# Where the low parts of split weights begin in SBUF: 64 bytes further for the stationary operand only

## The chip, the core and the metric

The kernel runs on one core of one Trainium2 chip. The time is the device time of one execution in microseconds; a kernel's time is the median over its runs. Three runs of the kernel before gave 1090.84 us at the median, from 1089.98 to 1092.05 us.

## What is computed

Two layers of a sequence model on 256 tokens of width 1024, in float32. Each layer is a half-weighted SwiGLU feed-forward network, a mixer, and another half-weighted feed-forward network, each between RMS norms and with a residual. The mixer of the first layer joins a gated convolution of width 31 with a state-space scan; that of the second is dilated window attention in three groups of eight heads. Nearly all of the arithmetic is products of the 256-token activations with weight matrices:

```python
def swiglu(u, w1, w2):
    gate, up = jnp.split(u @ w1, 2, axis=-1)        # w1: 1024 x 5632
    return (jax.nn.silu(gate) * up) @ w2            # w2: 2816 x 1024
...
for i in range(DEPTH):                              # DEPTH = 2
    h = h + 0.5 * rms_norm(swiglu(rms_norm(h, g[0]), ffn_w1[i, 0], ffn_w2[i, 0]), g[1])
    u = rms_norm(h, g[2])
    m = conv_ssd_mixer(u, ...) if i % 2 == 0 else dilated_attention_mixer(u, ...)
    h = h + rms_norm(m, g[3])
    h = h + 0.5 * rms_norm(swiglu(rms_norm(h, g[4]), ffn_w1[i, 1], ffn_w2[i, 1]), g[5])
```

## The kernel before

The weights lie in HBM as units of 128 x 2048 float32, in the order of their use. `prefetch` (L608) loads a unit into a `raw` buffer, ScalarE copies it to `wh` rounded to the matmul's type fp32r, and VectorE (GpSimd for the units 38 to 54) writes the rest, `raw - wh`, to `wl`. `wh` is the high part, `wl` the low part. Activations are split the same way, so that a product takes three matmuls: high by high, high by low, low by high. There are four buffers each of `raw`, `wh` and `wl`.

A unit is read in one of two ways. `unit(inner)` (L626) hands both parts out as `[128, k, inner]`.

- **As the stationary operand**, where `inner` is 256. `by_parts` (L671) streams high and low part of an activation (512 columns) past a 128 x 128 block of `wh`, and then the high part alone (256 columns) past the block of `wl`. `feat_major` (L661) does the same in three matmuls of 256 columns.
- **As the moving operand**, where `inner` is 512 or 1024. `mm3` (L635) loads a 128 x 128 block of the activation's high part and streams 512 columns of `wh`, loads it again and streams 512 columns of `wl`, and loads the low part and streams `wh` once more. It is called from `tok_major` (L655; activation tiles named `x`) and `acc_pairs` (L687; the down projections, whose activation tiles are named `s`, `x` in the mixer's output). The trace names a matmul's moving operand first: `w<-x,wl` streams `x` past a stationary `wl`, and `a<-wl,s` streams `wl` past a stationary `s`.

Each matmul has a LDWEIGHTS of its own, and the load for the next matmul begins while the current one streams.

All operations are recorded first. A planner (`schedule`, L336) simulates the engines with costs and gives each operation its place in its engine's queue and each buffer its slot; `lay_out` (L442) then creates the large buffers one behind the other, and `issue` (L459) issues everything in the planned order from L466, which is why the profile puts everything at that line. `lay_out` creates all large buffers except those of `wl` first, then one tile of 64 bytes that nothing uses, and then the four `wl` buffers. The small tiles follow as they come up. In the built program every large buffer begins 128 bytes past a multiple of 512, and the four `wl` buffers (at 192192, 200384, 208576 and 216768 in a partition) begin 192 bytes past one: 64 bytes further than all others. Blocks within a buffer are cut at multiples of 512 bytes, so this holds for every operand of the matmuls above. Below, "at 64" is said of an operand that begins there, and "at 0" of one that begins as the others do.

Of the kernel before, what the change touches and what calls it, by code (L numbers as in the profile page):

```python
# [9 lines left out]
F32 = mybir.dt.float32  # L10
# [7 lines left out]
P = 128  # L18
# [146 lines left out]
class View:  # L165


    def __init__(self, buf, ap, path=()):
        self.buf, self.ap, self.path = buf, ap, path
# [27 lines left out]
        return np.unique(at // self.buf.grain).tolist()  # L197


LINE, LINES = 64, 512  # L200


class Buf:
    def __init__(self, kind, shape, dtype, index):
        self.kind, self.shape, self.dtype, self.index = kind, shape, dtype, index
        self.cols = int(np.prod(shape[1:]))
        self.grain = max(1, self.cols // 32)
        self.slot = self.real = None
        self.uses = set()
        self.writer, self.readers, self.users = {}, {}, {}  # L210

    def tile(self):
        if self.real is None:
            k = self.kind
            self.real = k.pool.tile(self.shape, self.dtype, name=f"{k.name}_{self.index}", tag=f"{k.name}{self.slot}", bufs=1)
        return self.real


class Kind:


    def __init__(self, pool, name, count, psum):
        self.pool, self.name, self.count, self.psum = pool, name, count, psum
        self.bufs = []
        self.tenant = {}
        self.first = 0
        self.free_at = [0.0] * count
# [18 lines left out]
class Recorder:  # L246
# [8 lines left out]
        for e in ("tensor", "vector", "scalar", "gpsimd", "sync"):  # L255
            setattr(self, e, Engine(self, e))

    def kind(self, pool, name, count, psum=False):
        self.kinds[name] = Kind(pool, name, count, psum)

    def tile(self, name, shape, dtype=F32):
        kind = self.kinds[name]
        buf = Buf(kind, list(shape), dtype, len(kind.bufs))
        kind.bufs.append(buf)
        return View(buf, self.like(buf.shape, dtype))
# [176 lines left out]
    def lay_out(self, order):  # L442

        first = {}
        for o in order:
            for b in o.bufs:
                if not b.kind.psum:
                    first.setdefault((b.kind.name, b.slot), b)
        size = lambda b: b.cols * mybir.dt.size(b.dtype)
        large = [b for b in first.values() if size(b) % LINES == 0]  # L450
        for b in large:
            if b.kind.name != "wl":
                b.tile()
        next(iter(first.values())).kind.pool.tile([P, LINE // 4], F32, name="line", tag="line", bufs=1)
        for b in large:
            if b.kind.name == "wl":
                b.tile()

    def issue(self):  # L459
        real = lambda a: a.placed() if isinstance(a, View) else a  # L460
        with self.tc.manual_schedule():
            order = self.schedule()
            self.lay_out(order)
            for o in order:
                f = getattr(getattr(self.tc.nc, o.engine), o.name)
                o.ins = f(*[real(a) for a in o.args], **{k: real(a) for k, a in o.kw.items()})  # L466
# [79 lines left out]
class Kernel:  # L546
    def __init__(self, ctx, tc, x, weights, w_dt, gains, chan, heads, dt_bias, consts, out):
        self.tc, self.nc = tc, Recorder(tc)
        self.weights, self.gains = weights, gains
        self.x, self.out = x, out  # L550
        self.n = 0
        self.next_unit = 0
        self.use_unit = 0
        self.units = {}
        self.bg = []
        nc = self.nc
        sb = ctx.enter_context(tc.tile_pool(name="sb", bufs=1))
        ps = ctx.enter_context(tc.tile_pool(name="ps", bufs=1, space=PSUM))
        kind = lambda name, count: nc.kind(sb, name, count)
        kinds = {"raw": RAW_BUFS, "wh": W_BUFS, "wl": W_BUFS, "g": 2, "junk": 2}  # L560
        for name, count in {**kinds, **SB_BUFS, **{f"m{n}": count for n, count in SMALL.items()}}.items():
            kind(name, count)
        for name, count in PS_BUFS.items():
            nc.kind(ps, name, count, psum=True)
        self.kind = kind

        self.h = [self.keep(f"h{t}", [P, D]) for t in range(NT)]
        self.ident = self.keep("ident", [P, P])
        self.order = self.keep("order", [P, 2, P])
        self.consts = consts  # L570
        self.gain0 = self.keep("gain0", [P, KB])
        self.mhalf = self.keep("mhalf", [P, 1])
        nc.gpsimd.memset(self.mhalf, -0.5)
        self.mean = self.keep("mean", [P, P])
        nc.gpsimd.memset(self.mean, 1.0 / D)
        self.chan = self.keep("chan", [P, N_CHAN])
        self.heads = self.keep("heads", [P, 2, 16])
        self.dt_bias = self.keep("dtb", [16, 1])
        self.in_small = (chan, heads, dt_bias, w_dt)
# [46 lines left out]
    def unit(self, inner):  # L626
        i = self.use_unit
        self.use_unit += 1
        self.prefetch(i + 1 + AHEAD)
        hi, lo = self.units.pop(i)  # L630
        r = lambda a: a.rearrange("p (k n) -> p k n", n=inner)
        return r(hi), r(lo)

# [27 lines left out]
    def feat_major(self, ps, xT, unit, blk):  # L661
        hi, lo = unit
        for kb in range(KB):
            w = tuple(a[:, kb, blk * P : (blk + 1) * P] for a in (hi, lo))
            x = self.xb(xT, kb)
            mm = self.nc.tensor.matmul
            mm(ps, w[0], x[0], start=kb == 0, stop=False)
            mm(ps, w[0], x[1], start=False, stop=False)
            mm(ps, w[1], x[0], start=False, stop=kb == KB - 1)

    def by_parts(self, xT, unit, blk, bank, out, scale=1.0):  # L671

        nc = self.nc
        hi, lo = unit
        ps = self.ps([P, 2, SEQ], bank)
        for kb in range(KB):
            w = tuple(a[:, kb, blk * P : (blk + 1) * P] for a in (hi, lo))
            x = xT[kb // 2][:, kb % 2]
            nc.tensor.matmul(ps, w[0], x, start=kb == 0, stop=False)
            nc.tensor.matmul(ps[:, 0, :], w[1], x[:, 0, :], start=False, stop=kb == KB - 1)  # L680
        nc.scalar.activation(out, ps[:, 1, :], AF.Copy, scale=scale)
        if scale == 1.0:
            nc.vector.tensor_tensor(out=out, in0=ps[:, 0, :], in1=out, op=ALU.add)
        else:
            nc.vector.scalar_tensor_tensor(out=out, in0=ps[:, 0, :], scalar=scale, in1=out, op0=ALU.mult, op1=ALU.add)

    def acc_pairs(self, acc, lhs, unit, kk, start, stop, halves=(0, 1), **kw):  # L687
        hi, lo = unit
        for hf in halves:
            c = slice(hf * 512, (hf + 1) * 512)  # L690
            self.mm3(acc[hf], lhs, (hi[:, kk, c], lo[:, kk, c]), start, stop, **kw)
# [728 lines left out]
```

## Time and profile before

| | |
|---|---|
| median of three runs | 1090.84 us |
| the profiled execution's own time | 1091.85 us |
| its span on the core | 1090.1 us |
| TensorE (PE) matmuls, busy | 1072.9 us, 98% |
| weight loads (PEld), busy | 905.3 us, 83% |
| VectorE (DVE), busy | 765.8 us, 70% |
| ScalarE (ACT), busy | 656.4 us, 60% |
| GpSimd (POOL), busy | 142.2 us, 13% |
| 16 DMA engines, mean share | 51.3% (weights' queue) |
| mean granted TensorE clock | 0.999 of full speed |

The profile comes from one execution. Matmuls overlap in the pipeline, so a matmul's duration holds the time in which the next one already streams, and the ends are modelled; how much time one takes up is read from the starts of two of them in the timeline. A row of a group gives the operation, out<-in, the shape, how often it occurs, the busy time in us, the mean duration in ns, and the idle time before it with what ended that.

### The profile page before, as it was taken

To read this page: it belongs to the slowest core of one execution; us is meant where nothing else is said; L and a number is where in the kernel's file an instruction comes from. 1 tells how busy PE (TensorE), PEld (TensorE's weight loads), DVE (VectorE), ACT (ScalarE), POOL (GpSimd) and SP (SyncE) were. 2 spreads that over 40 slices of the span, in tenths; PEclk is the share of its full clock that TensorE was granted. 3 is DMA by queue.
4 is the path that set the end of the run, shared out by engine and by line. 5 is a ranking of instruction groups with operands and counts; after the bars stand their busy time and mean duration, and the time that the engine had idled before them with its cause. 6 is when DMAs were issued, how large, how long until landed. Compare 5 with 4: busy or idle time off the path is not lost.

```text
span 1090.1 us, 15864 instructions
## 1 busy us (share of the span) xinstructions
PE 1072.9 (98%) x5822; PEld 905.3 (83%) x5822; DVE 765.8 (70%) x1574; ACT 656.4 (60%) x1447; POOL 142.2 (13%) x136
## 2 busy tenths in 40 slices
PE   6999999999999999999999999999999999999997
PEld 5888888888878888888888888888888788888886
DVE  6756565889999885666677566568688868566563
ACT  7655555687676664655565555556576656465452
POOL 0000000069896000000000000000000400000000
PEclk9999999999999999999999999999999999999999
DMA  9755555445324576546537465554645235554621
GB/s 346 253 195 187 194 193 193 155 155 194 117 82 150 193 247 216 184 164 215 178 137 281 155 217 176 185 193 136 246 162 193 98 116 207 199 193 160 227 78 39
DMA packets 30206, 196.58 MB, mean 180 GB/s; under 512 B 3632, under 2 KB 4528, under 8 KB 7600
## 3 DMA queue, kind: packets, MB, share of 16 engines
q1 hardware_dynamic: 30128, 195.57, 51.3%
q8 instruction: 45, 0.74, 0.3%
q14 instruction: 33, 0.27, 0.1%
HBM read 194.51 MB, written 1.05 MB: 179 GB/s over the span
## 4 chain that ended last, share of the span: by engine, by line
PE 93%; DVE 3%; ACT 2%; DMA 1%; issue 0%; SPq 0%; DVEq 0%; POOLq 0%; POOL 0%; ACTq 0%
PE w L466 38%; PE a L466 32%; PE t L466 12%; PE c L466 12%; DVE c L466 1%; DVE t L466 1%; ACT wh L466 1%; DMA gain<-in_chan 1%; DVE s L466 0%; ACT junk L466 0%; SPq L466 0%; ACT c L466 0%; ACT t L466 0%; DVE m L466 0%; DVE h L466 0%
## 5 line engine op out<-in xcount | busy, mean ns | idle before, releaser
L466 DVE TENSOR_TENSOR wl<-raw,wh 128x512 fp32r<-128x512 f32 x642 | 415.0, 692 | 164.5 <-ACT wh L466 164.0
L466 ACT ACTIVATE wh<-raw 128x512 fp32r<-128x512 f32 x710 | 405.4, 626 | 205.4 <-PE a L466 83.3
L466 PE MATMUL w<-x,wh 128*128 128x512 f32 (+1 forms) x864 | 266.4, 365 | 0.9 <-DVE pt L466 0.7
L466 PE MATMUL a<-wh,s 128*128 128x512 f32 x800 | 256.4, 394 | 0.0
L466 PE MATMUL w<-x,wl 128*128 128x256 f32 x752 | 210.9, 281 | 0.0
L466 PEld LDWEIGHTS a<-wh,s 128*128 128x128 f32 x800 | 150.1, 188 | 35.8 <-ACT s L466 0.8
L466 PEld LDWEIGHTS w<-x,wh 128*128 128x128 f32 x864 | 154.6, 188 | 28.4 <-DVE pt L466 1.0
L466 PE MATMUL w<-wh,x 128*128 128x512 f32 x512 | 169.5, 405 | 1.9 <-ACT x L466 1.8
L466 PE MATMUL a<-wl,s 128*128 128x512 f32 x400 | 157.7, 394 | 0.0
L466 PEld LDWEIGHTS w<-x,wl 128*128 128x128 f32 x752 | 142.8, 190 | 2.1 <-issue 0.9
L466 POOL TENSOR_TENSOR m<-m,mhalf 128x1 f32<-128x1 f32 x28 | 18.0, 645 | 819.0 <-DVE m L466 818.9
L466 PE MATMUL t<-x,wh 128*128 128x512 f32 x336 | 118.5, 392 | 0.0
L466 PE MATMUL c<-x,wh 128*128 128x512 f32 x336 | 118.4, 392 | 0.0
L466 PEld LDWEIGHTS w<-wh,x 128*128 128x128 f32 x512 | 96.5, 190 | 24.6 <-ACT x L466 2.5
L466 PE MATMUL w<-wl,x 128*128 128x512 f32 x256 | 102.8, 403 | 0.0
L466 PE MATMUL t<-x,wl 128*128 128x256 f32 x336 | 94.0, 280 | 0.0
L466 PE MATMUL c<-x,wl 128*128 128x256 f32 x336 | 93.9, 280 | 0.0
L466 POOL TENSOR_TENSOR wl<-raw,wh 128x512 fp32r<-128x512 f32 x68 | 85.5, 1300 | 23.9 <-ACT wh L466 23.7
L466 PEld LDWEIGHTS a<-wl,s 128*128 128x128 f32 x400 | 75.1, 188 | 16.2
L466 ACT ACTIVATE sg<-w 128x256 f32<-128x256 f32 x96 | 36.6, 381 | 81.2 <-PE w L466 81.2
L466 DVE TENSOR_TENSOR sg<-w,sg 128x256 f32<-128x256 f32 x72 | 30.5, 424 | 78.0 <-ACT sg L466 75.4
L466 PEld LDWEIGHTS c<-x,wh 128*128 128x128 f32 x336 | 63.1, 188 | 13.5
(176 smaller groups left out, 1204.0 us busy)
## 6 DMA issues: line engine op xcount, KB each, us to landing
raw<-in_weights SPq DMA_DIRECT2D x176, 1024.0 KB, 4.8
g<-in_gains SPq DMA_DIRECT2D x11, 512.0 KB, 5.0
raw<-in_weights SPq DMA_DIRECT2D x4, 256.0 KB, 5.8
raw<-in_weights SPq DMA_DIRECT2D x2, 512.0 KB, 7.7
out<-h SPq DMA_DIRECT2D x4, 256.0 KB, 2.0
g<-in_consts SPq DMA_DIRECT2D x3, 192.0 KB, 2.4
h<-in_x SPq DMA_DIRECT2D x2, 256.0 KB, 2.8
h<-in_x SPq DMA_DIRECT2D x1, 512.0 KB, 6.5
```

What stands on the lines that cost most here:

```text
L466: o.ins = f(*[real(a) for a in o.args], **{k: real(a) for k, a in o.kw.items()})
```

## The change

The unused tile of 64 bytes goes. The `wl` buffers become 64 bytes larger (2064 instead of 2048 elements per partition), and each tenant of such a buffer gets a shift of its own: `unit` sets it to 16 elements, 64 bytes, where the unit is handed out with `inner == 256` (stationary) and to 0 otherwise (moving). Writing and reading both go through `Buf.tile`, so both see the shift.

```diff
-LINE, LINES = 64, 512
+LINE, LINES = 16, 512
...
     def tile(self):
         if self.real is None:
             k = self.kind
-            self.real = k.pool.tile(self.shape, self.dtype, name=f"{k.name}_{self.index}", tag=f"{k.name}{self.slot}", bufs=1)
-        return self.real
+            shape = [P, self.cols + k.margin] if k.margin else self.shape
+            self.real = k.pool.tile(shape, self.dtype, name=f"{k.name}_{self.index}", tag=f"{k.name}{self.slot}", bufs=1)
+        return self.real[:, self.shift : self.shift + self.cols] if self.kind.margin else self.real
...
-        size = lambda b: b.cols * mybir.dt.size(b.dtype)
-        large = [b for b in first.values() if size(b) % LINES == 0]
-        for b in large:
-            if b.kind.name != "wl":
+        size = lambda b: (b.cols + b.kind.margin) * mybir.dt.size(b.dtype)
+        small = sorted((b for b in first.values() if size(b) % LINES and not b.kind.margin), key=size, reverse=True)
+        for b in first.values():
+            if size(b) % LINES == 0:
                 b.tile()
-        next(iter(first.values())).kind.pool.tile([P, LINE // 4], F32, name="line", tag="line", bufs=1)
-        for b in large:
-            if b.kind.name == "wl":
+        for b in first.values():
+            if b.kind.margin:
                 b.tile()
+                room = -size(b) % LINES
+                for other in list(small):
+                    if (n := -(-size(other) // 32) * 32) <= room:
+                        other.tile()
+                        small.remove(other)
+                        room -= n
...
-        kind = lambda name, count: nc.kind(sb, name, count)
+        kind = lambda name, count: nc.kind(sb, name, count, margin=LINE if name == "wl" else 0)
...
         hi, lo = self.units.pop(i)
+
+        lo.buf.shift = LINE if inner == 256 else 0
```

In the built program the `wl` buffers now begin at 192128, 200832, 209536 and 218240, each 128 bytes past a multiple of 512, and small tiles (scalars and short rows of 4 to 128 bytes) fill the 448 bytes behind each. A stationary `wl` is read at 64, as before, in 1472 matmuls; a moving `wl` is read at 0 instead of 64, in 688 matmuls. No other large buffer moves. On all five engines the instructions, their order and the semaphores on which they wait are the same as before; addresses alone differ.

More of the change, by code (lines that the diff above doesn't have):

```diff
@@ L208, in __init__ @@
         self.slot = self.real = None
+        self.shift = 0
         self.uses = set()
@@ L214, in tile, with __init__ @@
             k = self.kind
-            self.real = k.pool.tile(self.shape, self.dtype, name=f"{k.name}_{self.index}", tag=f"{k.name}{self.slot}", bufs=1)
-        return self.real
+            shape = [P, self.cols + k.margin] if k.margin else self.shape
+            self.real = k.pool.tile(shape, self.dtype, name=f"{k.name}_{self.index}", tag=f"{k.name}{self.slot}", bufs=1)
+        return self.real[:, self.shift : self.shift + self.cols] if self.kind.margin else self.real
 class Kind:
-    def __init__(self, pool, name, count, psum):
-        self.pool, self.name, self.count, self.psum = pool, name, count, psum
+    def __init__(self, pool, name, count, psum, margin):
+        self.pool, self.name, self.count, self.psum, self.margin = pool, name, count, psum, margin
         self.bufs = []
@@ L256, in __init__, with kind @@
             setattr(self, e, Engine(self, e))
-    def kind(self, pool, name, count, psum=False):
-        self.kinds[name] = Kind(pool, name, count, psum)
+    def kind(self, pool, name, count, psum=False, margin=0):
+        self.kinds[name] = Kind(pool, name, count, psum, margin)
     def tile(self, name, shape, dtype=F32):
```

## The prediction

> **What bounds the kernel now.** I read the page first, for the engine that sets the end.
>
> ```profile
> span 1090.1 us, 15864 instructions
> PE 1072.9 (98%) x5822; PEld 905.3 (83%) x5822; DVE 765.8 (70%) x1574; ACT 656.4 (60%) x1447; POOL 142.2 (13%) x136
> ...
> PE 93%; DVE 3%; ACT 2%; DMA 1%; issue 0%; SPq 0%; DVEq 0%; POOLq 0%; POOL 0%; ACTq 0%
> PE w L466 38%; PE a L466 32%; PE t L466 12%; PE c L466 12%; DVE c L466 1%; DVE t L466 1%; ACT wh L466 1%; DMA gain<-in_chan 1%; DVE s L466 0%; ACT junk L466 0%; SPq L466 0%; ACT c L466 0%; ACT t L466 0%; DVE m L466 0%; DVE h L466 0%
> ```
>
> TensorE is busy for 98% of the span, and 93% of the chain that ended last is matmuls. So a change counts here only by what it does to the time that a matmul takes up in an unbroken stream. Next came the groups of TensorE with their shapes kept apart. These are the matmuls that touch a split weight (some small groups of the mixers left out).
>
> ```profile
> L466 PE MATMUL a<-wh,s 128*128 128x512 f32 x800 | 256.4, 394 | 0.0
> L466 PE MATMUL w<-x,wh 128*128 128x512 f32 x640 | 225.0, 393 | 0.0
> L466 PE MATMUL w<-x,wl 128*128 128x256 f32 x752 | 210.9, 281 | 0.0
> L466 PE MATMUL w<-wh,x 128*128 128x512 f32 x512 | 169.5, 405 | 1.9 <-ACT x L466 1.8
> L466 PE MATMUL a<-wl,s 128*128 128x512 f32 x400 | 157.7, 394 | 0.0
> L466 PE MATMUL t<-x,wh 128*128 128x512 f32 x336 | 118.5, 392 | 0.0
> ...
> L466 PE MATMUL w<-wl,x 128*128 128x512 f32 x256 | 102.8, 403 | 0.0
> ...
> L466 PE MATMUL a<-wh,x 128*128 128x512 f32 x64 | 21.3, 403 | 0.0
> ...
> L466 PE MATMUL a<-wl,x 128*128 128x512 f32 x32 | 12.7, 397 | 0.0
> ```
>
> The reader is to see two things: the groups hardly wait (idle 0.0 to 1.9 us), and the moving `wl`, which the change concerns, occurs 400 + 256 + 32 = 688 times. Durations overlap, so for the time that a matmul takes up I read the timeline of one passage of a feed-forward stage, from a pair of blocks in `by_parts` to the end of the down projection behind it. The rows are the first of `by_parts`, the first and the second of the down projection, and the first behind it.
>
> ```profile
> 82.06 0.39 PE L466 MATMUL t<-x,wh 128*128 128x512 f32 x1
> 82.29 0.28 PE L466 MATMUL t<-x,wl 128*128 128x256 f32 x1
> ...
> 87.61 0.40 PE L466 MATMUL a<-wh,s 128*128 128x512 f32 x1
> 87.84 0.39 PE L466 MATMUL a<-wl,s 128*128 128x512 f32 x1
> ...
> 93.17 0.39 PE L466 MATMUL w<-x,wh 128*128 128x512 f32 x1
> ```
>
> From 82.06 to 87.61 us stand 16 pairs of a 512- and a 256-column matmul: 5.55 us / 16 = 346.9 ns a pair. From 87.61 to 93.17 us stand 24 matmuls of 512 columns, 16 that move `wh` and 8 that move `wl`: 5.56 us / 24 = 231.7 ns each. That is the stretch that the change touches. The 688 moving `wl` take 688 x 231.7 ns = 159 us, 15% of the span, and the triples that they stand in, 3 x 688 matmuls, 478 us.
>
> **The change part by part.**
>
> *The stationary `wl`* stays at 64, in 1472 matmuls, and reads the same data against the same streams: nothing.
>
> *The moving `wl`* goes from 64 to 0, where `wh` lies already. The trace therefore holds both cases side by side, in the same triples, with the same stationary blocks: `a<-wl,s` streams from 64 and takes 394 ns, `a<-wh,s` streams from 0 and takes 394 ns. Both are rounded, so they differ by less than 1 ns. In the tok_major groups the pairs are 403 against 405 and 397 against 403; the `wh` row there holds the first matmul of each group, which has waited (1.9 us of idle time), so these pairs say no more than the first, and I take that one. If a moving `wl` at 0 behaves as `wh` does at 0, the sum is 688 x 0 = 0, with 688 x 1 ns = 0.7 us either way from the rounding.
>
> That is a comparison within a triple, and it leaves one thing open: whether one operand's place costs its neighbour time. So I looked for a row in which only the place of the operands against each other changes. The step sizes in the mixer have one. Their stationary block is 16 columns, 64 bytes, and eight such blocks lie one behind the other in 512 bytes, while 256 columns of `x` stream from 0 each time. The two answers below are for the first two blocks (while they stream, blocks at 0, 64 and 128 are loaded) and for four later ones (loads at 192 to 448), each with minimum, median and maximum of the duration; the maxima of 362 and 360 are the first matmul of each stretch, which has waited.
>
> ```profile
> L466 PE MATMUL w<-x,wdth x4: 282/282/362, 223.4 to 224.0; 128*16 128x256 f32 x4
> L466 PE MATMUL w<-x,wdtl x2: 282/282/283, 223.7 to 224.1; 128*16 128x256 f32 x2
> ...
> L466 PE MATMUL w<-x,wdth x8: 276/276/360, 225.2 to 226.4; 128*16 128x256 f32 x8
> L466 PE MATMUL w<-x,wdtl x4: 276/276/276, 225.5 to 226.5; 128*16 128x256 f32 x4
> ```
>
> The same matmul takes 282 ns with its neighbour's weights at 0 to 128 bytes from the stream's beginning, and 276 ns with them further on. So a load seems to cost the stream up to 6 ns where the two lie close, though a short wait stands between the two stretches and could be the reason instead. A 128-column block is 512 bytes, so its load passes through all eight places whatever it begins with, and a shift can only move the moment at which the two meet. That is why I expect far less than 6 ns of a shift of 64 bytes, and why the equal 394 ns of the two rows don't surprise me.
>
> The Trainium skill, page "TensorE: Matmul & The Clock Gate", section "Step-by-step: what each phase is for", states that TensorE has two independent read ports and that loading the next weights does not steal read bandwidth from the running matmul. By that rule no address changes anything and the sum is exactly 0; the 282 and 276 ns speak against it as a whole. Whether it holds for 128-column blocks no row here decides.
>
> *The bounds.* Below: a 512-column stream in `by_parts`, whose neighbour's load is at 64, takes 392 ns (`t<-x,wh`) against 394 ns in the triples, so an arrangement exists in which it is 2 ns shorter. If the triples' shift against each other is what they pay for, all three matmuls gain: 3 x 688 x 2 ns = 4.1 us less. Above: the step sizes' 6 ns for each moving `wl` that now begins where its neighbour's load begins: 688 x 6 ns = 4.1 us more.
>
> *Writing `wl`.* VectorE and GpSimd now write the moving units to 0.
>
> ```profile
> L466 DVE TENSOR_TENSOR wl<-raw,wh 128x512 fp32r<-128x512 f32 x640 | 412.6, 691 | 164.5 <-ACT wh L466 164.0
> L466 DVE TENSOR_TENSOR s<-cv,s 128x512 fp32r<-128x512 f32 x36 | 24.7, 686 | 0.7 <-ACT s L466 0.7
> ```
>
> The same operation to a tile at 0 takes 686 ns against 691 ns: at most 5 ns less in each of 640 instructions, 3.2 us of VectorE's time for all of them, and under half of that for the units that move. It is covered: these instructions idle for 164.5 us, 164.0 of it waiting for ScalarE's `wh`, and `wl` is not in the chain. Without that cover it would be a gain of some 1 us. Small tiles at new addresses are read by a few short instructions each; nothing in the chain above 1% reads them.
>
> **The sum.** 0 for the stationary parts, 0 +- 0.7 us for the moving ones, 0 for VectorE. The profiled execution took 1091.85 us (span 1090.1), 1.0 us over the median of 1090.84, so the forecast for the median is 1090.84 + 0 = 1090.8 us. A measurement of this kernel can tell about 0.2%, 2.2 us, from no change; 0.7 us is inside that.
>
> **The rivals.**
>
> *Faster: the triple as a whole pays for the shift.* Durations in the down projection are not constant: its matmuls take 387 to 402 ns in one passage although nothing waits, while those of `by_parts` keep to 392 or 393.
>
> ```profile
> L466 PE MATMUL a<-wh,s x15: 387/395/402, 87.6 to 92.5; 128*128 128x512 f32 x15
> L466 PE MATMUL a<-wl,s x8: 388/394/398, 87.8 to 92.7; 128*128 128x512 f32 x8
> ```
>
> So something carries over from one matmul to the next there, and the third operand at 64 in each triple may be what stirs it; in that case equal means of `wh` and `wl` prove nothing, because both share the cost. With all three at 0 the stream could settle at `by_parts`' 392 ns: -4.1 us, 1086.7 us. Against it: `by_parts` itself mixes both places (its load of `wl` at 64, that of `wh` at 0) and is steady.
>
> *Slower: a collision at the beginning of the stream.* While a moving `wl` streams, the block for the next matmul is loaded from 0. Before, the two begin 64 bytes apart; now both begin at 0, and if the load holds the stream up where they begin together, each of 688 matmuls pays up to the 6 ns of the step sizes: +4.1 us, 1094.9 us. It decides from 2.2 us / 688 = 3.2 ns per matmul on. Against it: `wh` at 0 is in that very position in the same triples and shows 394 ns too.
>
> *The change doesn't do what it says:* it would, if a unit with `inner == 256` were moved anywhere or its writer kept another shift. In the built program all 1472 stationary `wl` are at 64 and all 688 moving ones at 0, so I give this nothing beyond the case of no change.
>
> **How the numbers follow.** No measurable change: 0.46, because it is what the paired rows say. Faster: 0.37; the scatter of 387 to 402 ns shows that time is there to be had, and 2 ns on 2064 matmuls is enough. Slower: 0.17, which needs more than half of the price of the step sizes while `wh` already stands in the same place for none. The range goes from 1085.9 us (the faster case and 0.8 us for the scatter of a median) to 1094.0 us (the no-change case with its rounding, and the greater part of the slower one), which leaves about 2 in 10 outside; the no-change case by itself spans 1089 to 1093 us.
>
> **What would show it.** In the profile after, `a<-wl,s` and `a<-wh,s` at 394 ns each, and 5.56 us for a passage of 24 matmuls between two stretches of `by_parts`, would show the forecast right. At 392 ns for both and 5.51 us the faster rival is right, at 400 ns for `wl` alone (5.61 us) the slower. `by_parts` must stay at 346.9 ns a pair, and `w<-x,wl` at 281 ns; if they move, the stationary parts were not left alone. If the span moves and none of these rows does, the reason lies with an engine that I gave nothing.

## The result and the profile after

The changed kernel takes 1084.32 us at the median of six runs (1084.09 to 1085.6), the kernel before 1091.14 us in six runs beside it. The ratio is 0.9939, with a 95% interval from 0.9929 to 0.9949: 6.8 us faster, and below the range that was forecast. The profiled execution took 1084.34 us, against 1091.85 us before. The page of after, in the lines that answer to those of before:

```profile
span 1082.5 us, 15864 instructions
PE 1064.8 (98%) x5822; PEld 903.6 (83%) x5822; DVE 765.1 (71%) x1574; ACT 656.2 (61%) x1447; POOL 142.3 (13%) x136
...
PE 93%; DVE 3%; ACT 2%; DMA 1%; issue 0%; SPq 0%; DVEq 0%; POOLq 0%; POOL 0%; ACTq 0%
```

The span is 7.6 us shorter, TensorE's busy time 8.1 us, and TensorE is still 93% of the chain. Its weight loads (PEld) are 1.7 us shorter; no other engine moved by as much as 1 us. The groups of TensorE in after, with shapes kept apart:

```profile
L473 PE MATMUL a<-wh,s 128*128 128x512 f32 x800 | 253.2, 391 | 0.0
L473 PE MATMUL w<-x,wh 128*128 128x512 f32 x640 | 225.0, 393 | 0.0
L473 PE MATMUL w<-x,wl 128*128 128x256 f32 x752 | 210.9, 281 | 0.0
L473 PE MATMUL w<-wh,x 128*128 128x512 f32 x512 | 167.3, 401 | 2.3 <-ACT x L473 2.2
L473 PE MATMUL a<-wl,s 128*128 128x512 f32 x400 | 156.6, 391 | 0.0
L473 PE MATMUL t<-x,wh 128*128 128x512 f32 x336 | 118.5, 392 | 0.0
...
L473 PE MATMUL w<-wl,x 128*128 128x512 f32 x256 | 101.8, 400 | 0.0
...
L473 PE MATMUL a<-wh,x 128*128 128x512 f32 x64 | 21.1, 400 | 0.0
...
L473 PE MATMUL a<-wl,x 128*128 128x512 f32 x32 | 12.6, 394 | 0.0
```

Two things are to be seen. The groups with a stationary weight (`w<-x,wh`, `w<-x,wl`, `t<-x,wh`) show the same figures as before. And in the triples the moving `wh`, which the change does not touch, got shorter as the moving `wl` did: both go from 394 to 391 ns. The six groups of the triples lose 3.2 + 2.2 + 1.1 + 1.0 + 0.2 + 0.1 = 7.8 us, which accounts for the whole of the span's 7.6 us. The passage of a feed-forward stage in after (first of `by_parts`, first of the down projection, first behind it):

```profile
80.59 0.39 PE L473 MATMUL t<-x,wh 128*128 128x512 f32 x1
...
86.14 0.40 PE L473 MATMUL a<-wh,s 128*128 128x512 f32 x1
...
91.62 0.39 PE L473 MATMUL w<-x,wh 128*128 128x512 f32 x1
```

The 16 pairs take 5.55 us as before, 346.9 ns a pair. The 24 matmuls of the triples take 5.48 us, 228.3 ns each, against 231.7 ns before.

What changed within a triple is best seen in a longer unbroken run of them, the output projection of the first mixer. The rows of before from 362 to 372 us, with the least, the median and the greatest duration in ns, and then the first and the last moving `wl` of the timeline there:

```profile
L466 PE MATMUL a<-wh,s x30: 387/394/402, 361.9 to 371.9; 128*128 128x512 f32 x30
L466 PE MATMUL a<-wl,s x15: 388/395/398, 361.7 to 371.4; 128*128 128x512 f32 x15
```

```profile
361.69 0.40 PE L466 MATMUL a<-wl,s 128*128 128x512 f32 x1
...
371.44 0.40 PE L466 MATMUL a<-wl,s 128*128 128x512 f32 x1
```

The same in after:

```profile
L473 PE MATMUL a<-wh,s x31: 389/389/389, 361.8 to 372.0; 128*128 128x512 f32 x31
L473 PE MATMUL a<-wl,s x15: 389/389/389, 362.2 to 371.7; 128*128 128x512 f32 x15
```

```profile
362.22 0.39 PE L473 MATMUL a<-wl,s 128*128 128x512 f32 x1
...
371.74 0.39 PE L473 MATMUL a<-wl,s 128*128 128x512 f32 x1
```

Before, durations scatter from 387 to 402 ns although nothing waits; after, all 46 are 389 ns. Before, 14 triples take 9.75 us, 9.75 / 42 = 232.1 ns a matmul; after, 9.52 / 42 = 226.7 ns. A step, from the start of one matmul to that of the next, is 226 or 227 ns in this run of after. Below, such a run is called settled. The run of before never settles: its steps go from 224 to 241 ns, in a cycle that repeats every 15 matmuls (five triples). A run can need some matmuls to settle: the passage of after that begins at 86.14 us has steps of 235, 234, 235, 225, 230, 236, 229, 232 and 231 ns before it keeps to 226 or 227 ns.

That gives the size. In a passage of 24 matmuls the first nine gain nothing, and the passage gains 5.56 - 5.48 = 0.08 us. Only 576 of the 2064 matmuls of triples stand in passages of just this length; if all 2064 / 24 = 86 parts of 24 gained as much, it would be 6.9 us. Added up over the steps behind all 2064 in the two traces, the triples take 7.5 us less, beside 6.8 us in the medians and 7.6 us in the two profiled spans.

### The profile page after: what moved, and what is told of

It reads as the page before. It is cut to its first block, busy times and chain, and to the rows that moved or that the text cites. A ratio compares the mean times of both kernels' runs of the same rounds, so it can differ in the third digit from the quotient of the medians.

```text
span 1082.5 us, 15864 instructions
## 1 busy us (share of the span) xinstructions
PE 1064.8 (98%) x5822; PEld 903.6 (83%) x5822; DVE 765.1 (71%) x1574; ACT 656.2 (61%) x1447; POOL 142.3 (13%) x136
## 4 chain that ended last, share of the span: by engine, by line
PE 93%; DVE 3%; ACT 2%; DMA 1%; issue 0%; SPq 0%; DVEq 0%; POOLq 0%; POOL 0%; ACTq 0%
PE w L473 38%; PE a L473 31%; PE t L473 12%; PE c L473 12%; DVE c L473 1%; DVE t L473 1%; ACT wh L473 1%; DMA gain<-in_chan 1%; DVE s L473 0%; ACT junk L473 0%; SPq L473 0%; ACT c L473 0%; ACT t L473 0%; DVE m L473 0%; DVE h L473 0%
## 5 line engine op out<-in xcount | busy, mean ns | idle before, releaser
L473 PE MATMUL a<-wh,s 128*128 128x512 f32 x800 | 253.2, 391 | 0.0
L473 PE MATMUL w<-wh,x 128*128 128x512 f32 x512 | 167.3, 401 | 2.3 <-ACT x L473 2.2
```

## The experiments

Two theories stood at the start. The first, the faster rival of the prediction carried further: a run of triples settles if no operand of it begins at another place than the rest, and it is the whole run that pays. The main rival: what counts is each moving stream's place against the block that is loaded while it streams, so that streams that all begin at one place help only if that place is the load's. A third was that the new layout (small tiles between the `wl` buffers) did it. Addresses alone differ in all kernels, except that e4_steps256 also cuts one DMA in two.

**The moving part undone.** e9_undo keeps the new layout and reads the moving `wl` at 64 again.

```diff
-        lo.buf.shift = LINE if inner == 256 else 0
+        lo.buf.shift = LINE
```

> The changed kernel with its new layout (larger low-part buffers, small tiles behind them), but a shift of 64 in every use, as before the change. If the place of the moving low part is the whole cause: the kernel before, 1091.5 us, 24 in 5.56 us. If the new places of the small tiles have a part in it: less than that.

It took 1091.2 us, ratio to before 0.9999 [0.999, 1.0008]. Its groups:

```profile
L473 PE MATMUL a<-wh,s 128*128 128x512 f32 x800 | 256.4, 394 | 0.0
...
L473 PE MATMUL a<-wl,s 128*128 128x512 f32 x400 | 157.7, 394 | 0.0
```

Both are before's rows to the digit. The place of the moving `wl` is the whole of the change's effect; of the layout nothing is seen, to about 0.1%.

**All at 0.** e1_all0 takes the shift from the stationary `wl` too.

```diff
-        lo.buf.shift = LINE if inner == 256 else 0
+        lo.buf.shift = 0
```

> The changed kernel, but a stationary low part lies at 0 too, so that every operand of the split matmuls begins at 0. Theory (settling): a stream and the load beside it slide against each other until they no longer collide, and they settle only if each matmul has the same arrangement as the last; the moved triples are as in the changed kernel (passage of 24 in 5.49 us, long runs at 226.7 ns a matmul), and the pair in by_parts, now 346.7 ns, shows what its shift of 64 is worth, probably 1 to 4 ns more a pair, 1.4 to 5.8 us: 1086 to 1090 us. Rival (a wl moved from 64 is slow by its own place): the same for the triples, and nothing for the pairs, 1084.3 us. Rival (the small tiles' new places made the gain): 1084.3 us, nothing differs.

It took 1092.74 us, ratio 1.0012 [1.0003, 1.0022]. The triples settle as in after, and `by_parts` got slower. Its group, and then its run of triples:

```profile
L473 PE MATMUL t<-x,wh 128*128 128x512 f32 x336 | 120.6, 398 | 0.0
```

```profile
L473 PE MATMUL a<-wh,s x31: 389/389/389, 361.6 to 371.8; 128*128 128x512 f32 x31
L473 PE MATMUL a<-wl,s x15: 389/389/389, 361.9 to 371.4; 128*128 128x512 f32 x15
```

The 16 pairs of the passage take 5.65 us, 353.1 ns a pair against 346.9: 6.2 ns on some 1300 pairs is 8 us, and e1_all0 is 8.4 us over the changed kernel; 1 to 4 ns had been expected. So one buffer wants two places: 64 as the stationary operand, 0 as the moving one, and each use is worth 7 to 8 us by itself.

**The moving `wl` at 256.** e3_moved256 moves it away from `wh` again, by 256 bytes.

```diff
-margin=LINE if name == "wl" else 0)
+margin=4 * LINE if name == "wl" else 0)
...
-        lo.buf.shift = LINE if inner == 256 else 0
+        lo.buf.shift = LINE if inner == 256 else 4 * LINE
```

> The changed kernel with the moving low part at 256 bytes instead of 0 (stationary at 64 as before). Settling: one matmul of three differs from its neighbours again, no long run at 226.7 ns, 24 in 5.53 to 5.60 us, 1088 to 1094 us. Rival (a place of 64 is slow by itself, being no multiple of 128 or 256 from where buffers begin): 256 is a multiple of both, 24 in 5.49 us, 1084.3 us. Rival (nearness of stream and load costs): 256 is as far as can be, so the moving low part should be cheaper than wh, at or below 226.7 ns.

It took 1084.99 us, ratio 0.9941 [0.9926, 0.9956], the changed kernel's time. Its run of triples:

```profile
L473 PE MATMUL a<-wh,s x31: 389/389/389, 361.7 to 371.9; 128*128 128x512 f32 x31
L473 PE MATMUL a<-wl,s x15: 389/389/389, 361.9 to 371.4; 128*128 128x512 f32 x15
```

It settles at 389 ns just as at 0. One operand that begins elsewhere does not in itself keep a run from settling; 256 bytes count as no difference.

**The moving `wl` at 128.** e5_moved128 has 2 * LINE in the same two places.

> The changed kernel with the moving low part at 128 bytes (0 in the changed kernel, 64 in the one before; at 256 it settled as at 0). Theory (repeat of 128): the streams of a triple disturb each other only where their beginnings differ by an odd multiple of 64 bytes: long runs at 226.7 ns, 24 in 5.49 us, 1084.5 us. Rival (repeat of 256): 128 is the worst place, 24 in 5.56 us or more, 1091 us or more.

It took 1098.83 us, ratio 1.0064 [1.0041, 1.0087], 14.5 us slower than the changed kernel. The run of triples, and then the timeline of pairs early in the program (one, and the 15th behind it) and later (one, and the eighth behind it):

```profile
L473 PE MATMUL a<-wh,s x30: 392/395/398, 361.7 to 371.8; 128*128 128x512 f32 x30
L473 PE MATMUL a<-wl,s x15: 395/395/395, 362.2 to 372.0; 128*128 128x512 f32 x15
```

```profile
42.23 0.39 PE L473 MATMUL t<-x,wh 128*128 128x512 f32 x1
...
47.43 0.39 PE L473 MATMUL c<-x,wh 128*128 128x512 f32 x1
...
64.63 0.40 PE L473 MATMUL t<-x,wh 128*128 128x512 f32 x1
...
67.46 0.40 PE L473 MATMUL c<-x,wh 128*128 128x512 f32 x1
```

The triples run at 233.3 ns (14 of them in 9.80 us). The pairs tell more. Their operands stand where they stand in after. Up to the first down projection's triples, at 48 us, a pair takes (47.43 - 42.23) / 15 = 346.7 ns, as in after; behind them (67.46 - 64.63) / 8 = 353.8 ns. Of the 157 groups of eight pairs whose starts the trace has unbroken, 116 run at 353 ns. Nearly all others run at 346 to 347 ns. They stand in the mixers and at the beginning of each feed-forward network. In the first network the pairs slow down behind the first run of the down projection's triples, in the three later ones only behind the second, and from there on they stay slow to the network's end. The timeline of two groups of eight pairs in the second network, one before it slows down and one behind (each by its first row and the first row behind it):

```profile
432.19 0.39 PE L473 MATMUL w<-x,wh 128*128 128x512 f32 x1
...
434.96 0.39 PE L473 MATMUL t<-x,wh 128*128 128x512 f32 x1
...
479.92 0.40 PE L473 MATMUL w<-x,wh 128*128 128x512 f32 x1
...
482.74 0.40 PE L473 MATMUL w<-x,wh 128*128 128x512 f32 x1
```

They take 2.77 and 2.82 us, 346 and 353 ns a pair. In the built program both groups read and write the very same addresses, so no operand's place, in whatever buffer, is the difference between them. What differs is what went before, and the slow pace lasts through operations which the edit does not touch. It makes up 116 x 8 x 6.6 ns = 6.1 us of the 14.5; the rest lies in the triples themselves. No run rules out that what the other engines do meanwhile has a part in it.

**All moving weights at 64.** e2_weights64 starts from before and puts `wh` behind the unused tile as well, so that every moving weight streams from 64 while the activations' blocks are loaded from 0.

```diff
-            if b.kind.name != "wl":
+            if b.kind.name not in ("wh", "wl"):
...
-            if b.kind.name == "wl":
+            if b.kind.name in ("wh", "wl"):
```

> The kernel before, with both parts of the weights at 64 in every use: in the triples all three moving operands begin at 64 and the blocks loaded beside them at 0. Settling: all three matmuls of a triple have one arrangement again, so the stream settles, at 226.7 ns or near it, and a passage of 24 takes 5.45 to 5.52 us; the moved part gains its 7 us back. Rival (a place of 64 is slow by itself): all three matmuls are slow, 24 in 5.56 us or more. Rival (a stream must begin where the load beside it begins): no settling either, 5.56 us or more. In by_parts both loads are at 64 against a stream at 0; no number for its pair from either theory, 343 to 350 ns.

It took 1094.79 us, ratio 1.0035 [1.0021, 1.005]; the stationary `wh` and `wl` stand alike in it too, so its pairs pay as e1_all0's do (353.8 ns, outside the 343 to 350 that were expected). Its run of triples:

```profile
L466 PE MATMUL a<-wh,s x30: 392/393/394, 361.8 to 371.7; 128*128 128x512 f32 x30
L466 PE MATMUL a<-wl,s x16: 388/388/388, 361.6 to 371.9; 128*128 128x512 f32 x16
```

The three streams of a triple are alike now, and still the run does not come to 389 ns: it repeats with each triple (steps of 226, 229 and 232 ns), 228.9 ns on average (15 triples in 10.30 us). That is between before and after, and speaks for the rival: the place against the load counts.

**The same at 128.** e10_weights128 is e2_weights64 with an unused tile of 128 bytes.

```diff
-LINE, LINES = 64, 512
+LINE, LINES = 128, 512
```

> The kernel before with both parts of the weights at 128 in every use. All three streams of a triple begin at the same place again, 128 bytes from the blocks loaded beside them (at 64 it was 229.0 ns a matmul, at 0 it is 226.7). Theory A (only the difference between the streams of a triple counts, repeating every 256 bytes): 226.7 to 229 ns, 24 in 5.50 us or less. Theory B (the difference between each stream and the load beside it counts): the worst place of all, as a low part at 128 among high parts at 0 was with 233.3 ns; all three pay, 24 in 5.60 us or more. The pairs in by_parts have both loads at 128: if two loads at one place are what costs there, 353 ns as at 0 and at 64.

It took 1096.97 us, ratio 1.0053 [1.0033, 1.0073]. Its run of triples:

```profile
L466 PE MATMUL a<-wh,s x30: 392/395/398, 361.8 to 371.9; 128*128 128x512 f32 x30
L466 PE MATMUL a<-wl,s x14: 392/395/398, 362.3 to 371.4; 128*128 128x512 f32 x14
```

All streams alike, and 233.1 ns a matmul (15 triples in 10.49 us), no better than before's 232.1 with unlike streams. The first theory, by which only a difference between the streams counts, falls. Its pairs, 16 in 5.625 us or 351.6 ns each, are not quite at the 353 ns that were expected if two blocks at one place are what costs.

**Streams and loads at 64.** e12_weights_s64 is e2_weights64 with the activations `s` moved along; the activations `x` stay at 0.

```diff
-            if b.kind.name not in ("wh", "wl"):
+            if b.kind.name not in ("wh", "wl", "s"):
...
-            if b.kind.name in ("wh", "wl"):
+            if b.kind.name in ("wh", "wl", "s"):
```

> All weights at 64 in every use, as in the run that took 1094.8 us, and the activation tiles s at 64 as well, while the tiles x stay at 0. In the down projections stream and load beside it then begin at the same place, 64; where x is stationary the load is still at 0 against streams at 64. Theory (a stream settles where it begins at the same place, modulo 256 bytes, as the block loaded beside it): long runs at 226.7 ns in the down projections, and 229.0 ns still where x is stationary; 400 triples x 7 ns = 2.8 us less than that run, 1092 us. Rival (the streams' own place of 64 costs): 229.0 ns in both, 1094.8 us.

It took 1093.63 us, ratio 1.0019 [1.0009, 1.0029]; its pairs pay as e2_weights64's do. Its run of triples with a stationary `s`, and then one with a stationary `x`:

```profile
L466 PE MATMUL a<-wh,s x30: 389/389/389, 362.0 to 371.8; 128*128 128x512 f32 x30
L466 PE MATMUL a<-wl,s x16: 389/389/389, 361.8 to 372.0; 128*128 128x512 f32 x16
```

```profile
L466 PE MATMUL w<-wh,x x23: 388/392/398, 391.1 to 398.7; 128*128 128x512 f32 x23
L466 PE MATMUL w<-wl,x x11: 388/394/394, 391.6 to 398.4; 128*128 128x512 f32 x11
```

Where the loads moved along, the run settles at 389 ns and 226.7 ns a matmul (15 triples in 10.20 us). Where the load stayed at 0 and the stream is at 64, in the same program, the run repeats e2_weights64's pattern with each triple (steps of 226, 229 and 232 ns); the same run in the changed kernel has a median of 389 ns. Two other long runs with a stationary `x` in this program, and one in e2_weights64, stay at 233 ns instead, which is not explained. This is the test that tells the two theories apart, by the runs in the trace; the whole times, 1094.79 and 1093.63 us, hardly do. A run of triples settles where each stream begins at the place, modulo 256 bytes, of the block loaded beside it. At 0 and at 64, the two places that were run, the pace is the same.

**Only `wh` at 64.** e6_wh64 starts from before with `"wh"` in both conditions of `lay_out` in place of `"wl"`: two of the three streams of a triple at 64.

> The mirror of the kernel before: the high part begins at 64 in every use, the low part at 0. Theory (it is the difference between the streams of a triple): two streams at 64 and one at 0 do not settle, 24 in 5.54 us or more. Rival (each stream at 64 pays for itself against a load at 0): two of three pay, between the kernel before (one pays, 232.0 ns a matmul) and more, above 232 ns; but with all three at 64 it was 229.0 ns, which this rival can't explain. In by_parts the loads lie at 0 (beside 512 columns) and 64 (beside 256): if a shift between stream and load is what saves 6 ns a pair, the pair stays near 347 ns; if it must be the load beside the long stream, it goes to 353 ns.

It took 1093.32 us, ratio 1.0014 [1.0003, 1.0026]; its triples do not settle (397 ns for `wh`, 391 for `wl`). Its pairs in the timeline, in one stage and in the next (one and the eighth behind it, one and the 16th behind it):

```profile
65.99 0.40 PE L466 MATMUL t<-x,wh 128*128 128x512 f32 x1
...
68.82 0.40 PE L466 MATMUL c<-x,wh 128*128 128x512 f32 x1
...
77.24 0.40 PE L466 MATMUL w<-x,wh 128*128 128x512 f32 x1
...
82.69 0.39 PE L466 MATMUL t<-x,wh 128*128 128x512 f32 x1
```

With the operands' places, modulo 512 bytes, the same in both, a pair takes 2.83 / 8 = 353.8 ns in one and 5.45 / 16 = 340.6 ns in the other; through the program it changes between 340 and 350 or 353 ns, stretch by stretch. That was not expected. Here too groups of eight pairs with the very same addresses differ (341 ns from 77.24 us on, 350 ns from 96.52 us on), so the places don't set the pace alone.

**The step sizes turned.** e4_steps256 stores the eight 16-column blocks of the step sizes turned by four, so that the blocks that were loaded from 0 to 128 are loaded from 256 on.

```diff
-            wh, wl = (a[:, kb, :] for a in self.wdt)
+            wh, wl = (a[:, (kb + 4) % 8, :] for a in self.wdt)
...
-        nc.sync.dma_start(out=raw, in_=wdt)
+        for k in (0, 4):
+            nc.sync.dma_start(out=raw[:, 4 - k : 8 - k, :], in_=wdt[:, k : k + 4, :])
```

> The changed kernel, with the eight 64-byte blocks of the step sizes' weights stored turned by four places (one small load is cut in two for it): the first four streams load at 256 to 448 and the last four at 0 to 192. If the place decides, the first stretch takes 276 ns and the later one 282; if the short wait between them decides, 282 and 276 as before. Time as the changed kernel, 1084.3 us.

One execution, 1083.51 us. The two stretches in it:

```profile
L473 PE MATMUL w<-x,wdth x6: 282/283/362, 220.4 to 221.3; 128*16 128x256 f32 x6
...
L473 PE MATMUL w<-x,wdth x10: 276/276/361, 222.2 to 223.8; 128*16 128x256 f32 x10
```

And in the changed kernel, where nothing of these operations was edited:

```profile
L473 PE MATMUL w<-x,wdth x6: 276/276/361, 220.9 to 221.8; 128*16 128x256 f32 x6
...
L473 PE MATMUL w<-x,wdth x11: 276/276/361, 221.8 to 224.3; 128*16 128x256 f32 x11
```

The first stretch takes 282 ns in before, 276 ns in after with the same instructions at the same addresses, and 282 or 283 ns here with the loads far from the stream's beginning. By the numbers, the second of the two expected answers came: 282 and 276 ns, the wait. But in the changed kernel a wait stands there too, between two stretches of 276 ns, so the wait alone is not the reason either. The 6 ns do not go by the load's place; the same addresses ran at both paces, as pairs do in e5_moved128. The prediction's upper bound rested on that row, and it was misread.

**Other places for the stationary `wl`.** Three kernels change the changed kernel's stationary shift from 64 to 32, 48 and 128 bytes (`LINE // 2`, `12`, and `2 * LINE` with a larger margin), the moving `wl` staying at 0.

> The changed kernel with the stationary low part at 32 bytes instead of 64. At 0 the pair in by_parts takes 352.8 ns, at 64 it takes 346.7. If the saving grows with the bytes, 349.8 ns and 1088.5 us; if it takes a whole 64 bytes, 352.8 ns and 1092.5 us; if any shift will do, 346.7 ns and 1084.3 us.

> The changed kernel with the stationary low part at 48 bytes. The pair in by_parts took 352.8 ns at 0, 347.0 at 32, 346.7 at 64 and 350.0 at 128. If there is a smooth minimum between 32 and 64: 346 ns or less, 1083 to 1084 us; if 32 and 64 are on a floor: 347 ns, 1084.5 us.

> The changed kernel with the stationary low part at 128 bytes instead of 64. Theory (repeat of 128, as for the moving part): 128 is like 0, the pair in by_parts takes 352.8 ns and the kernel 1092.5 us. Rival (the load must be ahead of the stream by 64 bytes or more): 346.7 ns or less, 1084.3 us or less; a settled pair would take 340 ns, 9 us less than now.

They took 1084.76 us (ratio 0.9937 [0.9914, 0.9959]), 1084.23 us (0.9934 [0.9917, 0.995]) and 1087.84 us (0.9963 [0.9943, 0.9982]). In the passage, 16 pairs take 5.54, 5.54 and 5.60 us, 346 or 347 ns a pair for the first two and 350 ns for the third, which neither of its expected answers gave. With e1_all0's 353 ns that is a floor from 32 to 64 bytes with a rise on both sides. Nothing run here is told apart from the changed kernel as better.

## Why the prediction was wrong

It forecast 1090.8 us as the likeliest, with a range down to 1085.9; 1084.32 us came. By its own steps:

- **The stationary parts, VectorE and the layout at nothing: right.** `by_parts` stayed at 346.9 ns a pair and `w<-x,wl` at 281 ns. Writing `wl` took 690 ns a piece after 691, 0.3 us of VectorE's time in all, so little came of the 5 ns that tiles at 0 seemed to save; and e9_undo shows no effect of the small tiles.
- **The moving part, "if a moving `wl` at 0 behaves as `wh` does at 0, the sum is 688 x 0 = 0": this step failed.** Its condition held, `wl` behaves as `wh` does, in after as in before; the conclusion does not follow from it. The two rows stand in one sequence, and both held the cost: 394 and 394 ns became 391 and 391 ns, and e9_undo brings both back. The prediction said that equal means prove nothing if the triple shares the cost, and named the scatter of 387 to 402 ns as the sign of it, and still gave the equal means the greater chance. The scatter was the better witness: the run had not come to one pace.
- **The lower bound, 2 ns for each of 2064 matmuls: too small.** It took the settled duration from `by_parts`, 392 ns, a sequence of another kind. The triples settle at 389 ns and 226.7 ns a step. Measured over passages with their beginnings it is 7.6 us / 2064 = 3.7 ns a matmul of span. The faster rival had its mechanism right in that the run as a whole pays, and its price of 4.1 us too low. That the third operand only has to lie as the other two do is not enough (e10_weights128).
- **The slower rival: its sign was wrong.** In triples, a stream that begins together with the load beside it is the good case, not a collision (e12_weights_s64). That holds for triples only: pairs whose streams and loads all begin at 0 pay 6.2 ns (e1_all0). Its price came from the step sizes, which e4_steps256 and the changed kernel show to be no effect of the load's place.
- **The rule of the Trainium skill** (page "TensorE: Matmul & The Clock Gate", section "Step-by-step: what each phase is for") that the load of the next weights takes no read bandwidth from the running matmul would have made the change exactly 0. The traces disagree as far as times go: by addresses alone the 24 matmuls of a passage went from 5.56 to 5.48 us, and a pair from 346.9 to 353.1 ns. The 282 and 276 ns, which the prediction held against the rule, say nothing about it (e4_steps256). Whether read bandwidth is what is short no run here shows.

What stays open: what in the hardware carries the state from one matmul to the next; why streams at 64 against loads at 0 come to 228.9 ns in a period of three when all are alike; why pairs want their two blocks 32 to 64 bytes apart while triples want none; and why a few runs of triples with the same places stay at 233 ns. Pairs at 340 ns exist (e6_wh64); if all some 1300 pairs of the changed kernel ran so, (346.9 - 340.6) x 1300 = 8 us more would go, but no way to hold them there was tried.

## What to carry to other kernels

Two rows of one repeating sequence are no control for each other: an address that slows the sequence can slow all its members alike, as here (both 394 ns, then both 391), so compare whole sequences, and read scatter in durations where nothing waits as a cost that one of the operands may bring in. Where TensorE is the bound, the beginning of each moving stream against the block loaded beside it, modulo 256 bytes, is worth trying by itself, and separately for each kind of sequence, since here one buffer wanted 0 in one use and 64 in the other. Measure the sequences behind the edited one as well: they can slow down without being touched.

## What the runs showed of the hardware that was not expected

- **The pace does not follow from the addresses alone.** Within one program, pairs on the very same addresses ran at 346 or 353 ns (e5_moved128), and at 341 or 350 ns (e6_wh64); the step sizes, with the same addresses in two programs, ran at 282 or 276 ns (before and after). What ran before them differed.
- **Places count modulo 256 bytes** in the one pair of cases that tells: the moving `wl` at 256 gave the times of 0 (1084.99 and 1084.32 us), at 128 the worst (1098.83 us).
- **Addresses alone moved this kernel by 14.5 us**, 1.3%, between the places 0 and 128 of one operand (e5_moved128), with instructions, order and semaphores the same.
